# RWKV time mix: where a chunk's group norm is finished, which engine scales the state, and how the output projection is cut

## The chip, the core and the metric

One core of one Trainium2 chip runs the whole program in one launch. Its engines work side by side, each through a queue of its own in order: TensorE (PE, with its weight loads shown apart as PEld), VectorE (DVE), ScalarE (ACT), GpSimd (POOL) and SyncE (SP), which issues the DMAs. The metric is the device time of one execution in microseconds; the median of three runs is 2095.94 us.

## The reference, cut to what matters

The program is a stack of four layers over 256 tokens of width 1024. The change lies in the second layer's mixer, an RWKV-7 time mix with 16 heads of 64:

```python
def step(state, inp):
    r_t, w_t, k_t, v_t, kk_t, a_t = inp
    sa = jnp.einsum('bhvk,bhk->bhv', state, -kk_t)
    state = (state * w_t[:, :, None, :]
             + sa[..., None] * (kk_t * a_t)[:, :, None, :]
             + v_t[..., None] * k_t[:, :, None, :])
    y = jnp.einsum('bhvk,bhk->bhv', state, r_t)
    return state, y
...
mean = jnp.mean(y, axis=-1, keepdims=True)
var = jnp.mean(jnp.square(y - mean), axis=-1, keepdims=True)
yn = ((y - mean) * lax.rsqrt(var + LNX_EPS)).reshape(B, S, D)
yn = yn * lnx_w.astype(f32) + lnx_b.astype(f32)
bonus = (jnp.sum(r * k * r_k.astype(f32), axis=-1, keepdims=True) * v).reshape(B, S, D)
return ((yn + bonus).astype(x.dtype) * g) @ w_o
```

A group norm over each head's 64 values of `y`, gain and bias, a bonus, a gate `g`, and the output projection `w_o` (1024 by 1024). Everything is fp32.

## The kernel before

Activations lie with the feature on the partitions and the token along the free axis. Weights come as blocks of 128x1024, called units, through one queue of DMAs (`Stream`); `get()` hands out the next unit. A unit is either raw, so its matmuls are plain fp32, two rows on PE each (`add32`, L662, L665), or it is split by ScalarE (L378) and VectorE (L380) into a high and a low part of a rounded type, and a product is then three single-pass matmuls, one row each (`mm3`, L592 to L597). The split buffers are three; a unit's buffer goes back when the next unit is taken.

The recurrence is done in four chunks of 64 tokens (`rwkv_core`). `chain(c, fill)` (L1352) is the serial part. It multiplies the state `UV` by the queries of the correction (L1365) and copies the result to `Rs` (L1366, the first four head pairs on ScalarE, the rest on VectorE), solves within the chunk (L1378, copied to `UV` by L1380, half of the partitions on either engine), forms the next state (L1385, copied by L1388, which adds the old state scaled by the chunk's decay) and the outputs `y` (L1375, L1395), which ScalarE copies to `ym` (L1396). The scaled state `p0` is two multiplies of GpSimd (L1370), for chunks 1 and 2 alone, since chunk 0 starts from nothing and chunk 3 passes nothing on.

`outs(c, ym, zm)` (L1402) is the group norm of a chunk, in three steps: `center` (a matmul with the centring matrix, L1411; the square on ScalarE, L1412; the product with gate and gain on VectorE, L1413), `variance` (small matmuls, L461; an addition on VectorE, L1420; a power on GpSimd, L1422; a copy that spreads it, on ScalarE, L1423) and `scale` (four transposes, L1428; product and additions on VectorE, L1429 to L1438; a split of the upper half of the features, L566, L567). `chain` calls pieces of `fill` at three places (`more`): after the state's update, after the output matmuls, and after the last of those. So the group norm of chunk c - 1 runs beside chunk c, all three steps of it; that of chunk 3 runs after it in two halves. The tiles `ym`, `zm` and the scaled keys share the name `ymem` and its two buffers.

The projection follows. Its first four units are raw and go through twice, with tokens 0 to 191 and then 192 to 255; the other four are split and go through once with all 256 tokens, in the order of the units. All eight accumulate in four PSUM banks (`Acc`, L648). Each output feature block gets, per unit, a matmul of the given tokens (fp32) or three (single-pass). The tile framework sets the order on each engine from the order of the code and its own priorities; what it made is shown with the change.

Of the kernel before, what the change touches and what calls it, by code (L numbers as in the profile page):

```python
# [10 lines left out]
F32 = mybir.dt.float32  # L11
# [4 lines left out]
OP = mybir.AluOpType  # L16
# [3 lines left out]
P = 128  # L20
T = 256
# [122 lines left out]
def stream_units(inp):  # L144
# [15 lines left out]
    def qk(h):  # L160
        add(2048, lambda: _colunit(np.concatenate([wqkv[0][:, h * P:(h + 1) * P], wqkv[0][:, D + h * P:D + (h + 1) * P]], 1), 0))

    def v(j):
        add(2048, lambda: _colunit(wqkv[0], 2048 + 256 * j))
# [4 lines left out]
    for h in range(10):  # L169
        if h < 7:  # L170
            qk(h + 1)
        if h == 0:
            v(2)
            v(3)
        if h > 1:
            add(1024, lambda: wo[0][(h - 2) * P:(h - 1) * P])
# [276 lines left out]
def psum(k, tag, name=None):  # L453
    return k.ps.tile([P, 512], F32, name=tag, bufs={"acc": 4, "mm": 2, "tp": 2}[tag])
# [37 lines left out]
class Stat:  # L492
# [34 lines left out]
    def cols(self, tag="tp"):  # L527

        k, nc = self.k, self.k.nc
        if self.rs is not None:  # L530
            return self.rs
        if self.sums:
            self.i = self.n - len(self.sums)
            for x in self.sums:
                self.product(x, tag)
        while self.i < self.n:
            self.feed(self.h[:, self.i])
        m = self.m
        ms = k.small.tile([P, 2 * m], F32, name=f"ms{m}")
        nc.vector.tensor_scalar(ms[:, 2 * m - 2:], self.ps[:, 0:2 * m:m], 1e-6, None, op0=OP.add)  # L540
        if m == 2:

            nc.vector.scalar_tensor_tensor(ms[:, 0:2], ms[:, 2:4], 1e-6, self.ps[:, 1:4:2], op0=OP.mult, op1=OP.add)
        rs = k.small.tile([P, 2 * m], F32, name=f"rs{m}")
        nc.gpsimd.tensor_tensor(rs, ms, k.mh[:, 0:2 * m], op=OP.pow)
        self.rs = rs
        return rs
# [44 lines left out]
def mm3(k, out, w, x, start, stop, **kw):  # L592

    nc = k.nc
    nc.tensor.matmul(out, w[0], x[0], start=start, stop=False, **kw)  # L595
    nc.tensor.matmul(out, w[0], x[1], start=False, stop=False, **kw)  # L596
    nc.tensor.matmul(out, w[1], x[0], start=False, stop=stop, **kw)  # L597
# [50 lines left out]
class Acc:  # L648
# [3 lines left out]
        self.k, self.n, self.i = k, n, 0  # L652
        self.ps = [psum(k, "acc") for _ in range(4)]

    def add(self, unit, x):
        for m in range(8):
            w = [u[:, m * P:(m + 1) * P] for u in unit]
            mm3(self.k, self.ps[m // 2][:, (m % 2) * T:(m % 2 + 1) * T], w, x,
                self.i == 0 and m % 2 == 0, self.i == self.n - 1, skip_group_check=True)
        self.i += 1  # L660

# [318 lines left out]
def own(e):  # L980

    return slice(64 * e, 64 * e + 64)


def oth(e):

    return slice(64 - 64 * e, 128 - 64 * e)
# [250 lines left out]
def rwkv_core(k, h, es, R):  # L1238
    nc = k.nc
    pool = k.pool("rw_core", es=es)  # L1240
    flat = lambda t: t.rearrange("p a b -> p (a b)")
    t8 = lambda t: t.rearrange("p (h t) -> p h t", t=64)
    UV = pool.tile([P, 4, 8, 2, 64], F32, name="UV")
# [44 lines left out]
        GR.append(g)  # L1288

    def keys(c):  # L1290
        bk = pool.tile([P, 8, P], F32, name="ymem", bufs=2)
        for hp in range(8):
            nc.scalar.activation(bk[:, hp], R.BK[:, hp, c], AF.Copy, scale=R.PC[:, hp, c:c + 1])
        bt = pool.tile([P, 8, P], F32, name="BT", bufs=3)
        for half in range(2):
            ps = psum(k, "mm")
            for i in range(4):
                nc.tensor.transpose(ps[:, i * P:(i + 1) * P], bk[:, half * 4 + i], k.ident)
            nc.scalar.copy(bt[:, half * 4:half * 4 + 4], ps.rearrange("p (a t) -> p a t", a=4))
        BT.append(bt)  # L1300
# [23 lines left out]
    for c in range(4):  # L1324
        steps[c][0]()
        if c < 3:
            keys(c)
        if c < 2:
            spread_values(c + 2)
# [11 lines left out]
    def gate(j):  # L1341
        pg = psum(k, "mm")
        for m in range(2):
            hp = 2 * j + m
            nc.tensor.matmul(pg[:, m * T:(m + 1) * T], g2[:, hp * P:(hp + 1) * P], R.G1, start=True, stop=True)
            nc.scalar.activation(GL[:, hp], pg[:, m * T:(m + 1) * T], AF.Copy, scale=k.V("lnw", hp))
        nc.vector.tensor_tensor(flat(BG[:, 2 * j:2 * j + 2]), flat(BG[:, 2 * j:2 * j + 2]), pg, op=OP.mult)

    heads = [(hp, e) for hp in range(8) for e in range(2)]
    o = [None]  # L1350

    def chain(c, fill):  # L1352
        fill = iter(fill)
        more = lambda: [f() for f in next(fill, ())]
        cols = lambda hp: slice(hp * 64, hp * 64 + 64)
        Rs = pool.tile([P, 8, 64], F32, name="Rs")
        sides = [(half, slice(4 * half, 4 * half + 4), heads[8 * half:8 * half + 8]) for half in range(2)]
        at = lambda hp: cols(hp % 4)
        t4 = lambda x: t8(x)[:, 0:4]
        py = []  # L1360
        for half, hs, hd in sides:
            pr = psum(k, "acc")
            for hp, e in hd:
                r = oth(e) if c == 0 else slice(0, P)
                nc.tensor.matmul(pr[own(e), at(hp)], R.GTA[r, hp, c, e], UV[r, c, hp, e], start=True, stop=True)  # L1365
            both(half)(Rs[:, hs], t4(pr))  # L1366
        if 0 < c < 3:
            p0 = pool.tile([P, 8, 64], F32, name="PS0")
            for e in range(2):
                nc.gpsimd.tensor_tensor(p0[own(e)], UV[own(e), c, :, e], R.PC[own(e), :, c:c + 1].to_broadcast([64, 8, 64]), op=OP.mult)  # L1370
        for half, hs, hd in sides:
            py.append(psum(k, "acc"))
            if c > 0:
                for hp, e in hd:
                    nc.tensor.matmul(py[-1][own(e), at(hp)], UV[own(e), c, hp, e], R.RT[own(e), hp, c], start=hp % 4 == 0, stop=False, skip_group_check=True)  # L1375
            pu = psum(k, "acc")
            for hp, e in hd:
                nc.tensor.matmul(pu[own(e), at(hp)], XF[own(e), c * 8 + hp], Rs[own(e), hp], start=True, stop=True)  # L1378
            for e in range(2):
                both(e)(UV[own(e), c, hs, e], t4(pu)[own(e)])  # L1380
        if c < 3:
            for half, hs, hd in sides:
                ps = psum(k, "acc")
                for hp, e in hd:
                    nc.tensor.matmul(ps[own(e), at(hp)], BT[c][:, hp, own(e)], UV[:, c, hp, e], start=True, stop=True)  # L1385
                for e in range(2):
                    if c > 0:
                        nc.vector.tensor_tensor(UV[own(e), c + 1, hs, e], t4(ps)[own(e)], p0[own(e), hs], op=OP.add)  # L1388
                    else:
                        both(e)(UV[own(e), c + 1, hs, e], t4(ps)[own(e)])  # L1390
        more()
        ym = pool.tile([P, 2, 512], F32, name="ymem", bufs=2)
        for half, hs, hd in sides:
            for hp, e in hd:
                last = nc.tensor.matmul(py[half][own(e), at(hp)], UV[:, c, hp, e], GR[c][:, hp, e], start=c == 0, stop=True, skip_group_check=True)  # L1395
            nc.scalar.copy(ym[:, 0, half * 256:half * 256 + 256], py[half][:, 0:256])  # L1396
        more()
        with k.tc.issue_after(last.ins):
            more()
        return ym  # L1400

    def outs(c, ym, zm, h0=0, h1=8):  # L1402
# [37 lines left out]

        return center, variance, scale

    zmem = lambda: pool.tile([P, 2, 512], F32, name="ymem", bufs=2)
    ym = chain(0, [[lambda: gate(0), lambda: gate(1)], [lambda: gate(2), lambda: gate(3)]])
    k.st.free()
    for c in range(1, 4):
        f = outs(c - 1, ym, zmem())
        ym = chain(c, [[x] for x in f])
    zm = zmem()
    for f in zip(outs(3, ym, zm, 0, 4), outs(3, ym, zm, 4, 8)):  # L1450
        for x in f:
            x()

    acc = Acc(k, 12)
    us = [k.st.get() for _ in range(4)]
    for hp in range(4):
        acc.add32(us[hp], o[0][0][:, hp], slice(0, 192))
    for hp in range(4):
        acc.add32(us[hp], o[0][0][:, hp], slice(192, T))
        k.st.free(us[hp])  # L1460
    for hp in range(4, 8):
        acc.add(k.st.get(), [x[:, hp - 4] for x in o[0][1:]])
    return partial(acc.residual, h)


# [758 lines left out]
```

## Time and profile before

| | |
|---|---|
| runs | 2095.38, 2095.94, 2096.98 us |
| profiled execution | 2096.53 us, span 2094.7 us |
| PE busy | 2047.3 us (98%), 13856 matmuls |
| PEld busy | 1804.7 us (86%) |
| DVE busy | 1695.8 us (81%) |
| ACT busy | 1284.0 us (61%) |
| POOL busy | 134.3 us (6%) |
| mean granted clock of PE | 0.991 |

Times within the span count from its start. A busy time is the union of an engine's instructions; PE's rows overlap, since matmuls are pipelined, so what a matmul costs in a stream is the distance between starts, not its length. The granted clock is 1.00 at 2.4 GHz and 0.50 at 1.2 GHz. Idle time of an engine is put down to what ended it. The stretch of the change runs from about 485 to 562 us of the span.

### The profile page before, as it was taken

The page shows a single profiled execution, that of the slowest core. Times are in us where ns is not written, and L with a number is a line of the kernel's source. Part 1 is how long each engine was busy: PE and PEld are TensorE (multiplying, and loading weights), DVE is VectorE, ACT ScalarE, POOL GpSimd, SP SyncE. Part 2 cuts the span into 40 slices and gives each one's busy share as a digit, 9 for nine tenths or more (in the row PEclk, how much of TensorE's full clock was granted, in tenths as well). Part 3 has the DMA queues.
Part 4 walks back from the last instruction along what each step waited for, and adds up shares of the span by engine and source line. Part 5 has one row for each costly group of instructions (what it writes and reads, how often), then busy time and mean ns, then how long its engine had stood idle before and what let it go on. Part 6 is the DMA issues. An engine that isn't in the chain of part 4 may idle for free.

```text
span 2094.7 us, 36233 instructions
## 1 busy us (share of the span) xinstructions
PE 2047.3 (98%) x13856; PEld 1804.7 (86%) x13856; DVE 1695.8 (81%) x2417; ACT 1284.0 (61%) x1833; POOL 134.3 (6%) x133
## 2 busy tenths in 40 slices
PE   8999999998999999999999999999999999999997
PEld 7889998887899988999998878888888888887875
DVE  6879876665499767598877489999998989888987
ACT  6665453534364556454456477777777777777775
POOL 1011111101011100100000110000000000000002
PEclk9999999999999999999999999999999999999998
DMA  7348752230588634588854489998999999999991
GB/s 297 131 170 292 263 171 71 92 121 33 196 293 315 205 102 167 192 304 327 308 221 144 141 306 355 346 359 311 371 346 370 316 364 355 359 337 353 365 353 64
DMA packets 147910, 533.48 MB, mean 255 GB/s; under 512 B 16784, under 2 KB 17040, under 8 KB 147600
## 3 DMA queue, kind: packets, MB, share of 16 engines
q1 hardware_dynamic: 147728, 531.08, 69.6%
q8 instruction: 111, 1.82, 0.3%
q14 instruction: 71, 0.58, 0.1%
HBM read 529.97 MB, written 1.05 MB: 254 GB/s over the span
## 4 chain that ended last, share of the span: by engine, by line
PE 53%; DVE 3%; ACT 1%; issue 1%; DMA 0%; POOL 0%; ACTq 0%; POOLq 0%
PE acc L1958 8%; PE acc L1959 8%; PE acc L1957 8%; PE mm L1992 4%; PE mm L1991 4%; PE mm L1994 4%; PE mm L641 2%; PE acc L596 2%; PE acc L597 2%; PE acc L595 2%; DVE wlo L380 1%; PE mm L595 1%; PE mm L596 1%; PE mm L597 1%; PE tp L596 1%; PE tp L597 1%
## 5 line engine op out<-in xcount | busy, mean ns | idle before, releaser
L380 DVE TENSOR_TENSOR wlo<-raw,whi 128x1024 fp32r<-128x1024 f32 (+1 forms) x602 | 726.8, 1225 | 113.7 <-ACT whi L378 103.3
L378 ACT CAST whi<-raw 128x1024 fp32r<-128x1024 f32 (+1 forms) x608 | 622.6, 1041 | 249.3 <-PE acc L596 73.1
L1958 PE MATMUL acc<-wlo,XE 128*128 128x512 f32 x768 | 303.4, 395 | 1.0
L1957 PE MATMUL acc<-whi,XE 128*128 128x512 f32 x768 | 302.4, 395 | 0.0
L1959 PE MATMUL acc<-whi,XE 128*128 128x512 f32 x768 | 302.0, 393 | 0.0
L595 PE MATMUL mm<-Ahi,whi 128*128 128x256 f32 (+1 forms) x1016 | 290.8, 286 | 1.4 <-ACT whi L378 1.3
L597 PE MATMUL mm<-Ahi,wlo 128*128 128x256 f32 (+1 forms) x1016 | 289.0, 284 | 1.7 <-DVE wlo L380 1.7
L596 PE MATMUL mm<-Alo,whi 128*128 128x256 f32 (+1 forms) x1016 | 288.4, 284 | 0.7 <-DVE Alo L589 0.6
L595 PEld LDWEIGHTS mm<-Ahi,whi 128*128 128x128 f32 x1016 | 193.3, 190 | 4.9 <-issue 2.3
L597 PEld LDWEIGHTS mm<-Ahi,wlo 128*128 128x128 f32 x1016 | 193.2, 190 | 4.1 <-DVE wlo L380 2.2
L596 PEld LDWEIGHTS mm<-Alo,whi 128*128 128x128 f32 x1016 | 193.2, 190 | 1.7 <-DVE Alo L589 1.1
L380 DVE TENSOR_TENSOR wlo<-more,whi 128x1024 fp32r<-128x1024 f32 x150 | 177.8, 1219 | 9.6 <-ACT whi L378 6.8
L1958 PEld LDWEIGHTS acc<-wlo,XE 128*128 128x128 f32 x768 | 144.3, 188 | 37.4 <-DVE wlo L380 7.0
L378 ACT CAST whi<-more 128x1024 fp32r<-128x1024 f32 x150 | 154.3, 1049 | 33.5 <-PE acc L1959 22.2
L1957 PEld LDWEIGHTS acc<-whi,XE 128*128 128x128 f32 x768 | 144.4, 188 | 31.0
L1959 PEld LDWEIGHTS acc<-whi,XE 128*128 128x128 f32 x768 | 144.3, 188 | 30.5
L596 PE MATMUL acc<-fs,whi 128*128 128x256 f32 x544 | 152.6, 281 | 0.9 <-DVE fs L567 0.8
L597 PE MATMUL acc<-fs,wlo 128*128 128x256 f32 x544 | 152.9, 282 | 0.0
L595 PE MATMUL acc<-fs,whi 128*128 128x256 f32 x544 | 152.1, 282 | 0.4 <-ACT fs L566 0.4
L1992 PE MATMUL mm<-whi,h 128*128 128x512 f32 x384 | 152.1, 396 | 0.0
L1991 PE MATMUL mm<-whi,h 128*128 128x512 f32 x384 | 151.4, 394 | 0.0
L908 DVE SCALAR_TENSOR_TENSOR adaw<-adaw,adac 128x1024 f32<-128x1024 f32 x96 | 122.2, 1275 | 18.2 <-DMA adaw<-ada 17.8
(502 smaller groups left out, 3838.3 us busy)
## 6 DMA issues: line engine op xcount, KB each, us to landing
raw<-ws SPq DMA_DIRECT2D x658, 512.0 KB, 4.9
more<-ws SPq DMA_DIRECT2D x150, 512.0 KB, 5.7
adaw<-ada SPq DMA_DIRECT2D x96, 512.0 KB, 5.9
con<-ws SPq DMA_DIRECT2D x27, 512.0 KB, 5.5
tables<-ws SPq DMA_DIRECT2D x26, 512.0 KB, 5.6
rows<-ws SPq DMA_DIRECT2D x25, 512.0 KB, 5.6
XE<-ws SPq DMA_DIRECT2D x10, 512.0 KB, 5.1
raw<-ws SPq DMA_DIRECT2D x12, 256.0 KB, 5.2
```

The costliest lines, as they stand in the source:

```text
L378: self.ins[n] = nc.scalar.copy(hi[:, s], raw[:, s]).ins
L380: self.last = eng.tensor_tensor(lo[:, s], raw[:, s], hi[:, s].bitcast(F32), op=OP.subtract).ins
L595: nc.tensor.matmul(out, w[0], x[0], start=start, stop=False, **kw)
L596: nc.tensor.matmul(out, w[0], x[1], start=False, stop=False, **kw)
L597: nc.tensor.matmul(out, w[1], x[0], start=False, stop=stop, **kw)
L908: nc.vector.scalar_tensor_tensor(x, x, 1.0, c, op0=OP.mult, op1=OP.mult, accum_out=raw[:, j:j + 1])
L1957: nc.tensor.matmul(ps, xe[0][:, kt], w[0], start=(kt == 0), stop=False)
L1958: nc.tensor.matmul(ps, xe[0][:, kt], w[1], start=False, stop=False)
L1959: nc.tensor.matmul(ps, xe[1][:, kt], w[0], start=False, stop=(kt == KT - 1))
L1991: nc.tensor.matmul(py[e][q], x[0][i], w[0][i], start=(c == 0 and f + i == 0), stop=False)
L1992: nc.tensor.matmul(py[e][q], x[1][i], w[0][i], start=False, stop=False)
L1994: end = nc.tensor.matmul(py[e][q], x[0][i], w[1][i], start=False, stop=(c == 5 and f + i == 3))
```

## The change

`scale` of chunk c - 1 moves from the end of chain c to the first `more` of chain c + 1, ahead of `center` of chunk c; `scale` of chunk 2 follows chain 3, ahead of the group norm of chunk 3. The third place of `more` in `chain` goes. The two multiplies of L1370 go from GpSimd to VectorE. The tiles named `ymem` get a third buffer. In the projection the first seven units, four raw and three split, go through twice, with tokens 0 to 127 and then 128 to 255; the eighth goes once with all 256. For this `add` gets a slice of tokens, and the buffers of the three split units are taken out of the stream's hands (`kept`) and given back after their second pass. The four accumulators and the units' order are the same.

```diff
-    def add(self, unit, x):
+    def add(self, unit, x, s=slice(0, T)):
         for m in range(8):
             w = [u[:, m * P:(m + 1) * P] for u in unit]
-            mm3(self.k, self.ps[m // 2][:, (m % 2) * T:(m % 2 + 1) * T], w, x,
+            mm3(self.k, self.ps[m // 2][:, (m % 2) * T + s.start:(m % 2) * T + s.stop], w, [v[:, s] for v in x],
...
-        bk = pool.tile([P, 8, P], F32, name="ymem", bufs=2)
+        bk = pool.tile([P, 8, P], F32, name="ymem", bufs=3)
...
-                nc.gpsimd.tensor_tensor(p0[own(e)], UV[own(e), c, :, e], R.PC[own(e), :, c:c + 1].to_broadcast([64, 8, 64]), op=OP.mult)
+                nc.vector.tensor_tensor(p0[own(e)], UV[own(e), c, :, e], R.PC[own(e), :, c:c + 1].to_broadcast([64, 8, 64]), op=OP.mult)
...
         more()
-        with k.tc.issue_after(last.ins):
-            more()
         return ym
...
+    scale = []
     for c in range(1, 4):
         f = outs(c - 1, ym, zmem())
-        ym = chain(c, [[x] for x in f])
+        ym = chain(c, [scale + [f[0]], [f[1]]])
+        scale = [f[2]]
+    scale[0]()
     zm = zmem()
...
-    acc = Acc(k, 12)
-    us = [k.st.get() for _ in range(4)]
-    for hp in range(4):
-        acc.add32(us[hp], o[0][0][:, hp], slice(0, 192))
-    for hp in range(4):
-        acc.add32(us[hp], o[0][0][:, hp], slice(192, T))
-        k.st.free(us[hp])
-    for hp in range(4, 8):
-        acc.add(k.st.get(), [x[:, hp - 4] for x in o[0][1:]])
+    acc = Acc(k, 15)
+    us, kept = [k.st.get() for _ in range(4)], []
+    for _ in range(3):
+        us.append(k.st.get())
+        kept.append(k.st.spl.pop(k.st.cur - 1))
+    for s in (slice(0, P), slice(P, T)):
+        for hp in range(7):
+            if hp < 4:
+                acc.add32(us[hp], o[0][0][:, hp], s)
+            else:
+                acc.add(us[hp], [x[:, hp - 4] for x in o[0][1:]], s)
+            if s.start and hp < 4:
+                k.st.free(us[hp])
+            elif s.start:
+                t = kept.pop(0)
+                k.st.free_spl[t[0]].append(t)
+    acc.add(k.st.get(), [x[:, 3] for x in o[0][1:]])
```

The order on PE in chunk 2, before (-) and with the change (+). L1428, now L1426, are the transposes of a chunk's `scale`, L1411, now L1409, the centring, L1378 the products with `Rs`, L1385 the next state, L1395 the outputs:

```order
 L1375 MATMUL acc<-Ahi,UV 64x64 x8
-L1378 MATMUL acc<-Rs,xa 64x64 x5
-L1428 MATMUL tp<-ident,ymem 128x128 x4
-L1378 MATMUL acc<-Rs,xa 64x64 x3
+L1378 MATMUL acc<-Rs,xa 64x64 x8
 L1375 MATMUL acc<-Ahi,UV 64x64 x8
 L1378 MATMUL acc<-Rs,xa 64x64 x8
 L1385 MATMUL acc<-UV,BT 64x64 x8
-L1411 MATMUL mm<-ymem,con 128x512
-L1395 MATMUL acc<-GR,UV 64x64 x9
+L1426 MATMUL tp<-ident,ymem 128x128 x4
+L1409 MATMUL mm<-ymem,con 128x512
```

The four transposes of chunk 0 stood between the products with `Rs`, and stand behind the first half of the next state now.

The order on PE behind the last outputs of chunk 3, before, where L461 are the variances' small matmuls and L665 the fp32 matmuls of the projection:

```order
-L1411 MATMUL mm<-ymem,con 128x256 x2
-L1428 MATMUL tp<-ident,ymem 128x128 x4
-L461 MATMUL tp<-con,ymem 64x2 x8
-L665 MATMUL acc<-xv,raw_86 128x192
-L1428 MATMUL tp<-ident,ymem 128x128 x2
-L665 MATMUL acc<-xv,raw_86 128x192 x5
-L1428 MATMUL tp<-ident,ymem 128x128 x2
```

And the same place with the change:

```order
+L1409 MATMUL mm<-ymem,con 128x256 x2
+L665 MATMUL acc<-xv,raw_86 128x128 x4
+L1426 MATMUL tp<-ident,ymem 128x128 x4
+L461 MATMUL tp<-con,ymem 64x2 x4
+L665 MATMUL acc<-xv,raw_86 128x128 x4
+L461 MATMUL tp<-con,ymem 64x2 x4
+L665 MATMUL acc<-xv,raw_87 128x128 x3
+L1426 MATMUL tp<-ident,ymem 128x128 x2
+L665 MATMUL acc<-xv,raw_87 128x128 x3
+L1426 MATMUL tp<-ident,ymem 128x128 x2
```

The projection's first matmuls stood behind the transposes of chunk 2, and stand ahead of them now, with three more groups between the steps of chunk 3.

The order on VectorE in chunk 2. L1418 is the variance's addition, L1366 the copy to `Rs`, L1380 a copy of solved values, L380 a unit's low part:

```order
+L1418 TENSOR_SCALAR var<-tp 128x8
+L1370 TENSOR_TENSOR PS_5520<-UV,PC 64x512
 L1366 COPY Rs<-acc 128x256
-L1429 TENSOR_TENSOR ymem<-ymem,tp 128x512
+L1370 TENSOR_TENSOR PS_5520<-UV,PC 64x512
 L1380 COPY UV<-acc 64x4x64
-L1435 TENSOR_TENSOR xv<-ymem,BK 128x4x64
-L1438 TENSOR_TENSOR ymem<-ymem,BK 128x256
 L380 TENSOR_TENSOR wlo_91<-raw_89,whi_90 128x1024
+L1380 COPY UV<-acc 64x4x64
+L1388 TENSOR_TENSOR UV<-acc,PS_5520 64x4x64 x2
```

The state's two multiplies stand on either side of the copy to `Rs`, and chunk 0's product and additions have left the place ahead of the solved values. On SyncE's queue the order of the DMAs is the same.

## Rows read from the trace of the kernel before

**Rows 1.** Windows: us, busy PE, PEld, DVE, ACT, POOL, then clock, DMA share, GB/s
```profile
494.60:502.80 8.20, 7.82 (x181) 6.24 (x182) 4.40 (x8) 3.84 (x9) 0.19 (x1) 1.00 0.19 68
502.80:515.65 12.85, 9.30 (x187) 7.67 (x186) 7.02 (x16) 4.49 (x10) 3.74 (x3) 0.87 0.23 79
515.65:524.00 8.35, 6.79 (x158) 5.41 (x154) 5.48 (x12) 3.94 (x8) 1.64 (x1) 1.00 0.03 9
524.00:529.60 5.60, 2.63 (x25) 1.95 (x24) 2.39 (x7) 1.82 (x5) 2.08 (x2) 0.92 0.54 187
529.60:550.73 21.13, 21.00 (x135) 20.39 (x133) 3.45 (x10) 1.52 (x4) 1.68 (x2) 0.86 0.15 52
```

**Rows 2.** PE timeline, chunk 2: start us, length us, instruction, idle before
```profile
505.22 0.51 PE L1378 MATMUL acc<-Rs,xa 64*64 64x64 f32 x10
508.67 1.11 PE L1428 MATMUL tp<-ident,ymem 128*128 128x128 f32 x4 [2.94 <-ACT ymem L1423]
...
511.89 0.69 PE L1385 MATMUL acc<-UV,BT 128*64 128x64 f32 x16
```

**Rows 3.** Timeline of GpSimd (POOL) in chunk 2
```profile
504.08 2.16 POOL L1370 TENSOR_TENSOR PS<-UV,PC 64x512 f32<-64x512 f32 x2 [9.29 <-DVE UV L1388]
506.33 1.64 POOL L1422 TENSOR_TENSOR yrs<-var,mh 128x8 f32<-128x8 f32 x1
```

**Rows 4.** Timelines of VectorE (DVE) and ScalarE (ACT) in chunk 2
```profile
504.58 0.16 DVE L1420 TENSOR_SCALAR var<-tp 128x8 f32<-128x8 f32 x1
...
508.00 0.62 ACT L1423 COPY ymem<-yrs 128x512 f32<-128x512 f32 x1 [4.01 <-POOL yrs L1422]
```

**Rows 5.** Windows around the two falls of the clock, as rows 1
```profile
508.67:510.70 2.03, 2.03 (x22) 1.70 (x24) 0.69 (x1) 0.27 (x1) 0.00 (x0) 0.50 0.00 0
524.00:527.57 3.57, 1.14 (x6) 0.68 (x5) 1.05 (x3) 1.32 (x4) 1.64 (x1) 1.00 0.60 197
527.57:534.60 7.03, 6.35 (x35) 5.52 (x36) 3.52 (x10) 1.61 (x5) 2.12 (x2) 0.58 0.13 51
```

**Rows 6.** Timeline of PE, chunk 3 and the start of the projection
```profile
519.60 0.66 PE L1428 MATMUL tp<-ident,ymem 128*128 128x128 f32 x4 [1.42 <-ACT ymem L1423]
...
524.80 1.13 PE L1411 MATMUL mm<-ymem,con 128*128 128x256 f32 x4 [0.79 <-ACT ymem L1396]
527.57 0.66 PE L1428 MATMUL tp<-ident,ymem 128*128 128x128 f32 x4 [1.63 <-ACT ymem L1423]
528.15 0.40 PE L461 MATMUL tp<-con,ymem 128*64 128x2 f32 x8
...
529.62 1.01 PE L665 MATMUL acc<-xv,raw 128*128 128x192 f32 x2
...
531.24 3.41 PE L665 MATMUL acc<-xv,raw 128*128 128x192 f32 x10
```

**Rows 7.** Line L665 in two windows: rows, ns min/median/max, first and last start
```profile
L665 PE MATMUL acc<-xv,raw x48: 326/326/326, 535.7 to 543.3; 128*128 128x192 f32 x48
L665 PE MATMUL acc<-xv,raw x59: 275/275/275, 543.8 to 550.3; 128*128 128x64 f32 x59
```

**Rows 8.** Lines L596 and L1958, every third single-pass matmul, as rows 7
```profile
L596 PE MATMUL acc<-xb,whi x25: 283/283/283, 552.0 to 560.6; 128*128 128x256 f32 x25
L1958 PE MATMUL acc<-wlo,XE x11: 388/394/397, 1500.9 to 1507.8; 128*128 128x512 f32 x11
```

**Rows 9.** Weight loads (PEld) of the same two kinds, as rows 7
```profile
L665 PEld LDWEIGHTS acc<-xv,raw x59: 192/192/192, 543.9 to 550.4; 128*128 128x128 f32 x59
L596 PEld LDWEIGHTS acc<-xb,whi x26: 192/192/192, 551.9 to 560.9; 128*128 128x128 f32 x26
```

**Rows 10.** Timeline of VectorE in chunk 1
```profile
495.45 0.69 DVE L1347 TENSOR_TENSOR BK<-BK,mm 128x512 f32<-128x512 f32 x1 [1.92 <-ACT BK L1346]
```

**Rows 11.** Timelines of GpSimd and VectorE at the same moment, in the tail
```profile
531.69 1.01 POOL L1422 TENSOR_TENSOR yrs<-var,mh 128x4 f32<-128x4 f32 x1 [1.42 <-DVE var L1420]
...
531.94 0.42 DVE L1435 TENSOR_TENSOR xv<-ymem,BK 128x256 f32<-128x256 f32 x1
```

More of the change, by code (lines that the diff above doesn't have):

```diff
@@ L1391, in chain @@
         more()
-        ym = pool.tile([P, 2, 512], F32, name="ymem", bufs=2)
+        ym = pool.tile([P, 2, 512], F32, name="ymem", bufs=3)
         for half, hs, hd in sides:
@@ L1441, in outs @@
         return center, variance, scale
-    zmem = lambda: pool.tile([P, 2, 512], F32, name="ymem", bufs=2)
+    zmem = lambda: pool.tile([P, 2, 512], F32, name="ymem", bufs=3)
     ym = chain(0, [[lambda: gate(0), lambda: gate(1)], [lambda: gate(2), lambda: gate(3)]])
     k.st.free()
+    scale = []
     for c in range(1, 4):
         f = outs(c - 1, ym, zmem())
-        ym = chain(c, [[x] for x in f])
+        ym = chain(c, [scale + [f[0]], [f[1]]])
+        scale = [f[2]]
+    scale[0]()
     zm = zmem()
```

## The prediction, made before the changed kernel ran

> **What bounds the kernel now.** I read the page first: PE is busy for 98% of the span, so time comes only from places where PE stands still, runs at its lower clock, or has work that can be made shorter. Then the windows view, cut at the edges of the chunks of the recurrence and of the projection behind it [rows 1]. Chunk 1 takes 8.20 us, chunk 2 takes 12.85 and chunk 3 8.35, for the same number of matmuls, so 4 to 5 us of chunk 2 are a stall. Behind chunk 3 come 5.60 us with PE busy for 2.63, then the projection: 21.13 us of fp32 matmuls and 96 single-pass ones of 256 columns, 11.4 us at the pitch below.
>
> The timeline of PE names the stall of chunk 2: four transposes wait 2.94 us for ScalarE's copy, in the middle of the matmuls with `Rs` [rows 2]. GpSimd's timeline says why the copy is late: the power of chunk 0 runs from 506.33, behind two multiplies of 1.08 us each [rows 3], though its input left VectorE at 504.74 [rows 4]. The stall costs twice: after it the granted clock is 0.50 for 2.03 us [rows 5], so 1.2 GHz in place of 2.4. The same happens at the end: the transposes of chunk 2 wait 1.63 us, the first fp32 matmul of the projection starts at 529.62 [rows 6], and the clock averages 0.58 over the 7.03 us from those transposes on [rows 5]. Inside chunk 3 a wait of 1.42 us has the same cause [rows 6].
>
> Last, the pitch of the projection's matmuls (first start to last start). An fp32 matmul is two rows of PE. At 192 columns a row takes (543.3 - 535.7)/47 = 0.162 us, at 64 columns (550.3 - 543.8)/58 = 0.112 us [rows 7]. A third of the columns takes 70% of the time: something other than the columns bounds the narrow row. Single-pass matmuls: 256 columns take (560.6 - 552.0)/72 = 0.119 us (24 gaps of every third row), 512 columns (1507.8 - 1500.9)/30 = 0.230 us [rows 8].
>
> **The change, part by part.** I walk PE's new order with durations from these rows; each start is the later of the engine being free and the last input being ready.
>
> *Chunk 2.* GpSimd's two multiplies go, so the power starts at about 504.8 and ends 1.64 us later [rows 3], ScalarE's copy of 0.62 us [rows 4] ends near 507.2, and its copies of the solved values, queued behind it, let the state update start at about 508.0 in place of 511.89 [rows 2]. The transposes come after the first half of that update, where their input is ready, so nothing waits for them. A wait of some 1.4 us before the state update is what is left. From there to the end of the chunk the same matmuls took 3.76 us (511.89 to 515.65) [rows 1, 2], and the transposes add 0.6 [rows 6]. Chunk 2 comes to 9.5 us: **-3.35**.
>
> *VectorE's four new multiplies.* No row shows them there. The nearest is a multiply of as many elements a partition, 0.69 us [rows 10]; GpSimd's 1.08 [rows 3] is the other end. I take 0.69. In chunk 1 the pair lies in 1.92 us in which VectorE waits for ScalarE [rows 10]. In chunk 2 one stands ahead of VectorE's `Rs` copy and one behind; the copy comes 0.7 us later, when PE is still at the first half's matmuls, and the second ends near 506.7, before ScalarE's copy at 507.2. So they cost nothing; at 1.08 us each the second would end near 507.3 and still cost nothing. VectorE's second copy now stands behind a weight subtraction that waits for ScalarE's cast; it ends near 510.2, when PE is at the centring of chunk 1.
>
> The page "SBUF — State Buffer" of the Trainium skill (section "Who interferes with whom") says that a VectorE instruction with two SBUF inputs and a GpSimd instruction that reads SBUF shut each other out, which would put the second multiply behind the power and make chunk 2 about 0.7 us longer, the sum -4.15. Here a VectorE addition with two SBUF inputs ran its usual 0.42 us inside GpSimd's power of 1.01 us [rows 11], so the row speaks against it, and I leave it out.
>
> *Chunk 3.* The transposes of chunk 1 stand after the centring of chunk 2, so PE works where it waited 1.42 us [rows 6]. New: VectorE's `Rs` copy and the two halves of the solved values come behind more of its own work, about 0.25 us of waits, while the 6.79 us of busy PE [rows 1] hold some 0.2 that is chunk 2's. I take 6.8 in place of 8.35: **-1.55**.
>
> *Tail and fp32 part.* Before: 524.00 to 550.73, or 26.73 us [rows 1]. Now the first pass needs only chunks 0 and 1, and its fp32 matmuls stand between the last chunk's small steps. An fp32 matmul of 128 columns is bounded below by 256 stream steps of 0.162/384 = 0.108 us a row and by the narrow row's 0.112; I take 0.112, the larger, so 32 matmuls are 32 x 0.224 = 7.2 us a pass. Pass one: centring 1.1 [rows 6], matmuls 7.2, transposes and variances 1.9 (0.6, twice 0.3 and twice 0.35, by the rows of four and of eight at full clock [rows 6]), and waits of about 1.9 (the transposes of chunk 2 still wait 1.5 us, since four matmuls cover only 0.9 of a chain that takes 2.6 from variance to copy, and the first half of chunk 3 waits 0.4): 12.1. Pass two: 7.2. Together 19.3: **-7.45**. Of this 3.2 us are a better split (192 + 64 columns cost 0.324 + 0.224 a matmul, 128 + 128 cost 0.448); the rest are covered waits and the lower clock, during which twelve rows ran at 0.33 us [rows 6].
>
> *Single-pass part.* Three units are done twice with 128 columns: 144 matmuls for 72, and the last unit stays whole. This price decides, and no row before shows a single-pass matmul under 256 columns. Columns alone, from 0.119 and 0.230, give 0.064 us; the price of an fp32 matmul of that width, two rows, gives 0.224. I take 0.112, that of the 64-column fp32 row: it streams as long (64 columns at two steps), it loads as wide a weight, and the weight load takes 192 ns in both forms [rows 9]. So 144 x 0.112 = 16.1 against 72 x 0.119 = 8.6: **+7.5**. The halving buys nothing in these units.
>
> *At nothing:* the third `ymem` buffer (the keys of chunks 0 to 2 are scaled earlier, while PE has other work) and the later free of the three kept units: the last unit's split waits for the first of them, which comes two units of 24 x 0.112 and one of 24 x 0.119 before the end, 8.3 us, where it is 8.6 now. What is late next is the same first unit of the feed-forward.
>
> Sum: -3.35 - 1.55 - 7.45 + 7.5 = **-4.85 us**. The same walk with the order of before gives 528.4 for the first fp32 matmul, where the trace has 529.62: it leaves out the lower clock. So it holds to about 1.2 us at each end of the path. The profiled execution took 2096.53 us (span 2094.7); less 4.85 is 2091.7. It lies 0.6 above the median of the three runs, 2095.94, so the median to expect is **2091.1 us**. A measurement of this kernel can tell about 0.2%, 4.2 us, from no change; the forecast lies just beyond.
>
> **The rivals.**
> 1. *Narrow single-pass matmuls cost as much as fp32 ones.* Were a 128-column one to take 0.224 us, 144 of them cost 16.1 us more than I allow: +11.3, so 2107.2. It decides from 0.112 + 4.85/144 = 0.146 us upward. For it: the code keeps every narrow piece in fp32, and the trace is silent. Against: it is one row of PE at 256 and 512 columns, and follows the columns there [rows 8]. Chance 0.17.
> 2. *The floor of 0.112 belongs to fp32 alone*, and single-pass rows follow the columns: 0.064, a further -6.9, so 2084.2. Against it: equal weight-load rows [rows 9]. Chance 0.09.
> 3. *The cover fails.* The waits left in the tail (1.5 and 0.4 us) or the 1.4 of chunk 2 let the clock fall as now: as long as in the present tail, 6.8 us at half, costs 3.4; so 2094.5, no change. For it: two of three such stretches before had it. Against: PE did 1.14 us of work in the 3.57 before that fall [rows 5], and would do over half now; the wait of 1.42 in chunk 3 had no fall behind it. Chance 0.15.
> 4. *Weight loads do not lie beside a running matmul.* A load of 0.112 and a stream of 0.054 would add up to 0.166 us, +7.8, so 2098.9. The 64-column row has both parts and takes 0.112 [rows 7], so hardly. The page "TensorE: Matmul & The Clock Gate" of the Trainium skill (section "The mechanism") says that a weight load overlaps matmuls in flight only when the row group differs, which is this; the trace disagrees. Chance 0.03.
>
> That the change does not do what it says is out: the order shows every move.
>
> **How the numbers follow.** The forecast has 0.56 and its own range is 2088 to 2094 (1.2 us at either end of the walk, narrow rows between 0.105 and 0.120). Somewhat over half of it lies beyond 4.2 us: 0.31 faster, 0.25 same. Rival 2 adds 0.09 to faster, rival 3 gives 0.13 to same and 0.02 to slower, rivals 1 and 4 give 0.20 to slower. Faster 0.40, same 0.38, slower 0.22. For 8 in 10 the range must reach rival 1; rival 2 is left out: 2087 to 2108.
>
> **What would show it.** Chunk 2 from its first matmul to that of chunk 3 near 9.5 us, with no wait of PE for chunk 0's transposes; GpSimd with powers alone; the first fp32 matmul of 128 columns within 1.5 us of chunk 2's variance; a granted clock of 1.00 through the tail; rows of 0.112 us in both kinds of pass. Single-pass rows over 0.146 make the forecast wrong in sign, rows near 0.064 make it too small, a clock of 0.50 behind the tail's first wait is rival 3.

## The result and the profile after

| | before | after |
|---|---|---|
| median of 5 runs each, us | 2095.42 (2090.98 to 2096.98) | 2104.87 (2104.69 to 2109.65) |
| ratio, 95% interval | | 1.0057 [1.0046, 1.0069] |
| span of the profiled execution, us | 2094.7 | 2103.1 |
| mean granted clock | 0.991 | 0.987 |

The changed kernel is slower by 9.45 us, where 4.85 less were forecast. First the place that the forecast was about: the windows view of the changed kernel, cut at the same edges as [rows 1] (chunks 1, 2 and 3; the rest of the tail with the first fp32 pass; the first single-pass pass; the second fp32 pass; the second single-pass pass; the last unit). The columns are those of [rows 1].

```profile
508.45:517.60 9.15, 7.86 (x181) 6.25 (x182) 4.81 (x9) 4.40 (x11) 0.00 (x0) 1.00 0.19 61
517.60:526.95 9.35, 7.28 (x187) 6.15 (x185) 7.22 (x15) 3.07 (x6) 1.94 (x1) 1.00 0.31 101
526.95:533.95 7.00, 6.92 (x157) 5.54 (x155) 6.01 (x14) 3.88 (x9) 1.75 (x1) 1.00 0.26 95
533.95:545.80 11.85, 10.57 (x94) 9.64 (x93) 6.08 (x18) 3.75 (x10) 3.75 (x3) 1.00 0.14 46
545.80:553.80 8.00, 8.00 (x74) 8.00 (x74) 0.00 (x0) 0.00 (x0) 0.00 (x0) 1.00 0.01 2
553.80:561.00 7.20, 7.20 (x67) 7.20 (x66) 0.00 (x0) 0.00 (x0) 0.00 (x0) 1.00 0.49 151
561.00:568.95 7.95, 7.95 (x74) 7.95 (x73) 2.46 (x2) 2.10 (x2) 0.00 (x0) 1.00 0.86 308
568.95:571.95 3.00, 3.00 (x27) 2.96 (x25) 1.95 (x4) 1.87 (x3) 0.00 (x0) 1.00 0.65 212
```

These add up to 63.50 us. Before, the same work took 67.73: 56.13 from chunk 1 to the first single-pass matmul [rows 1], and 11.60 for the four single-pass units behind it. So 4.23 us are gained here, close to the forecast, at a granted clock of 1.00 throughout. The loss lies ahead of it. Chunk 1 starts at 508.45 in place of 494.60, behind the solves and queries (64x64 matmuls, L1265 and L461) and the keys. `keys(c)` makes a chunk's keys ready: ScalarE scales them into a `ymem` tile (eight instructions, L1293), PE transposes that (L1298), and ScalarE copies the result to `BT` (L1299). The windows of that stretch, first of the changed kernel, then of the one before:

```profile
457.35:460.00 2.65, 2.65 (x40) 2.56 (x40) 0.00 (x0) 2.65 (x10) 0.00 (x0) 1.00 0.53 196
460.00:465.15 5.15, 2.12 (x35) 1.81 (x33) 2.51 (x3) 5.04 (x15) 0.00 (x0) 1.00 0.00 1
466.10:500.20 34.10, 34.10 (x482) 32.11 (x480) 11.09 (x15) 5.38 (x11) 0.00 (x0) 0.50 0.01 2
500.20:508.45 8.25, 8.25 (x135) 6.68 (x134) 5.62 (x11) 6.72 (x18) 0.00 (x0) 1.00 0.01 2
```

```profile
459.70:465.15 5.45, 4.77 (x73) 4.37 (x72) 2.29 (x3) 5.36 (x16) 0.00 (x0) 1.00 0.27 96
465.15:494.60 29.45, 29.43 (x622) 26.16 (x622) 16.15 (x25) 14.97 (x40) 1.92 (x2) 1.00 0.01 3
```

From the first solve to chunk 1 the changed kernel takes 508.45 - 457.35 = 51.10 us, before 494.60 - 459.70 = 34.90: **16.2 us lost**. In 34.10 of the 51.10 us TensorE is busy all the time at a granted clock of 0.50, its level of 1.2 GHz. What came first is in the timeline of PE (changed kernel, then before; of this and the later timelines only the rows spoken of are shown):

```profile
460.23 1.90 PE L1265 MATMUL tp<-xa,Alo 64*64 64x64 f32 x32
465.16 1.25 PE L1298 MATMUL mm<-ident,ymem 128*128 128x128 f32 x8 [3.04 <-ACT BT L1299]
466.34 3.31 PE L1265 MATMUL tp<-xa,Alo 64*64 64x64 f32 x32
...
498.30 2.06 PE L1345 MATMUL mm<-G,raw 128*128 128x256 f32 x4
```

```profile
462.58 1.90 PE L1265 MATMUL tp<-xa,Alo 64*64 64x64 f32 x32
465.17 1.15 PE L1298 MATMUL mm<-ident,ymem 128*128 128x128 f32 x8 [0.70 <-ACT BT L1299]
466.25 1.90 PE L1265 MATMUL tp<-xa,Alo 64*64 64x64 f32 x32
```

The second chunk's key transposes wait 3.04 us for ScalarE in place of 0.70; behind the wait the same 32 matmuls take 3.31 us in place of 1.90, and the clock rises only near 500 us, at the end of the first matmuls with a 128x128 weight and 256 columns (L1345, in `gate`). ScalarE's timeline (changed kernel, then before) says why:

```profile
457.10 4.78 ACT L1293 ACTIVATE ymem<-BK,PC 128x128 f32<-128x128 f32 x16
461.90 0.59 ACT L1336 COPY vt<-acc 128x512 f32<-128x512 f32 x1
464.52 1.08 ACT L1299 COPY BT<-mm 128x512 f32<-128x512 f32 x2
```

```profile
459.45 2.45 ACT L1293 ACTIVATE ymem<-BK,PC 128x128 f32<-128x128 f32 x8
461.91 0.59 ACT L1336 COPY vt<-acc 128x512 f32<-128x512 f32 x1
464.53 1.08 ACT L1299 COPY BT<-mm 128x512 f32<-128x512 f32 x2
465.48 1.00 ACT L1293 ACTIVATE ymem<-BK,PC 128x128 f32<-128x128 f32 x3
```

With two `ymem` buffers the third chunk's keys had to wait for a buffer, so their eight scalings stood behind the first copies to `BT`. With three they are ready at once and stand ahead: 16 in one block, 2.3 us more before the copy that PE waits for.

The account: PE was 2.35 us earlier at the first solve in the changed kernel. Of this it had 0.73 at 331 us already (the same 64 matmuls of L461 start at 330.98 and, before, at 331.71); the rest comes from a stretch at half clock near 335 us, which the profiled execution of before has and this one has not (windows 320 to 340: 0.91 and 1.00). -2.35 + 16.2 - 4.23 is +9.6 us at the projection's end; the spans differ by 8.4, so 1.2 us come back behind it.

### The profile page after: what moved, and what is told of

It is laid out like the page before. It is cut to its first block, busy times and chain, and to the rows that moved or that the text cites. A ratio compares the mean times of both kernels' runs of the same rounds, so it can differ in the third digit from the quotient of the medians.

```text
span 2103.1 us, 36364 instructions
## 1 busy us (share of the span) xinstructions
PE 2057.2 (98%) x13928; PEld 1815.9 (86%) x13928; DVE 1700.3 (81%) x2421; ACT 1282.9 (61%) x1833; POOL 129.1 (6%) x129
## 5 line engine op out<-in xcount | busy, mean ns | idle before, releaser
L380 DVE TENSOR_TENSOR wlo<-raw,whi 128x1024 fp32r<-128x1024 f32 (+1 forms) x602 | 727.2, 1226 | 115.9 <-ACT whi L378 106.3
L596 PE MATMUL mm<-Alo,whi 128*128 128x256 f32 (+1 forms) x1016 | 288.0, 284 | 0.7 <-DVE Alo L589 0.6
L596 PEld LDWEIGHTS mm<-Alo,whi 128*128 128x128 f32 x1016 | 192.7, 190 | 1.7 <-DVE Alo L589 1.1
L380 DVE TENSOR_TENSOR wlo<-more,whi 128x1024 fp32r<-128x1024 f32 x150 | 177.9, 1220 | 9.6 <-ACT whi L378 6.8
L596 PE MATMUL acc<-fs,whi 128*128 128x256 f32 x544 | 152.7, 281 | 0.9 <-DVE fs L567 0.8
```

The costliest lines, as they stand in the source:

```text
L380: self.last = eng.tensor_tensor(lo[:, s], raw[:, s], hi[:, s].bitcast(F32), op=OP.subtract).ins
```

## The experiments

The theory: **the third buffer puts the third chunk's scalings ahead of the copy to `BT`; PE waits 3 us; the clock falls, and the 64x64 matmuls that follow do not bring it back.** The rivals: the narrow passes of the projection or VectorE's multiplies cost the time; the buffer itself does it in some other way; the long half clock came by chance. Times are medians; the kernel before ran beside each group: 2095.01 us (e1 to e4), 2094.82 (e5 to e8), 2094.16 (e9 to e11).

**e1_keys_two.** The keys rotate through two buffers; `ym` and `zm` take those in turn with a third of their own.

```diff
-        bk = pool.tile([P, 8, P], F32, name="ymem", bufs=3)
+        bk = pool.tile([P, 8, P], F32, name="ymem", bufs=2)
-        ym = pool.tile([P, 2, 512], F32, name="ymem", bufs=3)
+        ym = zmem()
-    zmem = lambda: pool.tile([P, 2, 512], F32, name="ymem", bufs=3)
+    third = [0]
+
+    def zmem():
+        third[0] += 1
+        if third[0] % 3 == 0:
+            return pool.tile([P, 2, 512], F32, name="ymx")
+        return pool.tile([P, 2, 512], F32, name="ymem", bufs=2)
```

> The changed kernel with the keys kept to two buffers as before: the third buffer goes only to the chain's outputs. Theory (the third buffer lets ScalarE scale two chunks of keys in one block, PE waits 3.04 us for BT, the clock falls to 0.50 and stays there for 34 us): no half clock between 465 and 500 us of the span, chunk 1 starts again near 494.6 us, and what is left of the change gains 4 to 5 us: about 2091 us. Rival (the narrow passes of the projection or VectorE's multiplies cost the time): as the changed kernel, about 2105 us. Rival (the long half clock came by chance and hangs on nothing in the kernel): either, with 2105 as likely as 2091.

Measured: 2090.69 us (2089.15 to 2093.28), ratio 0.9985 [0.9976, 0.9994]. The wait for `BT` is 0.71 us, and the windows show no half clock:

```profile
464.47 1.15 PE L1298 MATMUL mm<-ident,ymem 128*128 128x128 f32 x8 [0.71 <-ACT BT L1299]
```

```profile
457.70:466.00 8.30, 7.59 (x94) 6.54 (x93) 2.70 (x3) 8.17 (x24) 0.00 (x0) 1.00 0.24 89
466.00:500.00 34.00, 33.96 (x736) 29.49 (x736) 20.51 (x33) 15.88 (x42) 0.00 (x0) 1.00 0.06 18
```

Without the third buffer for the keys the change gives 4.3 us; 14.2 of the changed kernel's time hang on that one number.

**e2_third_buffer_alone.** The kernel before with `bufs=3` for `ymem` in its three places.

> The kernel before with the third ymem buffer and nothing else: 16 scalings of keys in one block on ScalarE. Theory: PE waits about 3 us for BT near 465 us, the granted clock is 0.50 from there for about 34 us, and the time is 12 to 16 us over before: 2107 to 2112 us. Rival (it is the projection or the multiplies): no change, 2095 us. Rival (chance): either.

Measured: 2111.55 us (2107.76 to 2112.86), ratio 1.0077 [1.0063, 1.0091]: 16.5 us lost. PE's timeline row of the wait, and the window behind it:

```profile
467.64 1.97 PE L1298 MATMUL mm<-ident,ymem 128*128 128x128 f32 x8 [3.06 <-ACT BT L1299]
```

```profile
467.20:504.70 37.50, 37.06 (x507) 34.77 (x508) 11.43 (x17) 7.42 (x15) 0.00 (x0) 0.50 0.01 2
```

All five executions take over 2107 us, where none of the kernel before takes over 2098, so it is not chance.

**e3_projection_alone.** The kernel before with the changed projection (and `add` with its slice), nothing else.

> The kernel before with the changed projection alone (seven units in two passes of 128 tokens), two buffers, group norm as before. Theory: the tail and the fp32 units gain about 7, the single-pass units cost 7.5: within 1 us of before, 2095 to 2097 us, clock 1.00 between 465 and 500. Rival (the projection is what cost the time): 2103 to 2106 us.

Measured: 2096.11 us (2093.60 to 2099.51), ratio 1.0010 [1.0001, 1.0019]. The narrow passes are not what cost 9 us; what they win in the fp32 units goes in the single-pass ones, about as the forecast's two terms had it (-7.45 and +7.5). In its trace the stretch from chunk 1 to the last single-pass matmul takes 69.1 us in place of 67.6, and the tail still has half clock (0.87 over 13.05 us from 522.50).

**e4_group_norm_alone.** e1 with the projection of before (`Acc(k, 12)`, 192 and 64 tokens, single-pass units whole).

> The moved group norm and VectorE's multiplies alone, keys in two buffers, projection as before (192 and 64 tokens, single-pass units whole). Theory: chunk 2 and chunk 3 gain 3.35 and 1.55 us, the tail is about as before: 2090 to 2092 us. Rival (the multiplies on VectorE or the later group norm cost more than they give): 2096 us or over.

Measured: 2088.07 us (2086.72 to 2089.73), ratio 0.9971 [0.9960, 0.9982]: 6.9 us, 2 more than expected. From chunk 1 to the last single-pass matmul its trace takes 61.8 us, before 67.6, so 5.8 are gained there, though the tail still has half clock (0.61 over 8.00 us from 518.00). Its profiled execution also lacks the half clock near 335 us, whose 3.4 us cost at most 1.7. The median of e1, which has the changed projection besides, is 2.6 us higher, and its trace takes 62.9 us for the stretch: on top of the moved group norm the projection as changed costs time (the two intervals overlap a little).

**e5_single_pass_whole.** e1 with the two passes for the fp32 units alone.

```diff
+    acc = Acc(k, 12)
+    us = [k.st.get() for _ in range(4)]
+    for s in (slice(0, P), slice(P, T)):
+        for hp in range(4):
+            acc.add32(us[hp], o[0][0][:, hp], s)
+            if s.start:
+                k.st.free(us[hp])
+    for hp in range(4, 8):
+        acc.add(k.st.get(), [x[:, hp - 4] for x in o[0][1:]])
```

> As e1_keys_two, but the four single-pass units are done whole, 256 columns a matmul; only the four fp32 units keep the two passes of 128. Theory (a single-pass matmul of 128 columns costs nearly as much as one of 256, so halving it buys nothing): 144 x 0.110 us become 72 x 0.119, 7.3 us less than e1: 2083 to 2084 us, 11 to 12 us under before. Rival (the three units in the first pass are needed as cover for the tail): the tail waits again, half of the gain is lost: 2087 us or over.

Measured: 2081.67 us (2081.18 to 2082.34), ratio 0.9935 [0.9923, 0.9948]: 13.2 us under before. Its windows of the tail with both fp32 passes, and of all four single-pass units:

```profile
519.85:538.60 18.75, 17.67 (x159) 16.73 (x157) 5.29 (x16) 3.39 (x10) 3.75 (x3) 1.00 0.27 87
538.60:550.20 11.60, 11.60 (x99) 11.59 (x97) 4.37 (x6) 3.96 (x5) 0.00 (x0) 1.00 0.77 267
```

The changed kernel takes 11.85 + 7.20 = 19.05 us for the first and 8.00 + 7.95 + 3.00 = 18.95 for the second. The single-pass units were not needed as cover: the fp32 pass of 128 tokens is enough.

**e6_keys_on_two_engines.** The changed kernel with three buffers, every second scaling of the keys on VectorE (`tensor_scalar`, L1294).

> The changed kernel with its third buffer kept, and every second scaling of the keys on VectorE, so that ScalarE has 4 where it had 8 ahead of BT. Theory (what lowers the clock is PE's wait for ScalarE, not the buffer as such): no wait over 1 us between 455 and 475 us, clock 1.00 through the solves, 2088 to 2092 us. Rival (the third buffer, or chance, or the projection): half clock from about 465 us, 2103 to 2107 us.

Measured: 2089.05 us (2087.98 to 2092.33), ratio 0.9972 [0.9961, 0.9983]. The timelines of VectorE and PE, and a window:

```profile
452.41 2.44 DVE L1294 TENSOR_SCALAR ymem<-BK,PC 128x128 f32<-128x128 f32 x12
464.13 1.09 PE L1301 MATMUL mm<-ident,ymem 128*128 128x128 f32 x8
```

```profile
460.00:500.00 40.00, 39.75 (x853) 35.26 (x850) 23.46 (x37) 20.17 (x48) 0.00 (x0) 1.00 0.10 29
```

Three buffers, no wait, no half clock: it is the wait and not the buffer as such.

**e7_full_matmuls_inside.** The changed kernel, with this behind `queries(0)`:

```diff
+        if c == 0:
+            px = psum(k, "mm")
+            for i in range(4):
+                nc.tensor.matmul(px[:, (i % 2) * T:(i % 2 + 1) * T], k.ident, R.BK[:, 2 * i:2 * i + 2, 0], start=True, stop=True)
```

> The changed kernel with four more fp32 matmuls of 128 rows, 128 weight columns and 256 columns (their result is not used) behind the first chunk's queries, inside the stretch at half clock, near 477 us. Theory (the clock stays low because 64x64 matmuls fill a quarter of the array, and full matmuls bring it back, as the first ones at 498 us do in the changed kernel): they take about 4.1 us, and the clock is 1.00 behind them; the 19 us that are left of the stretch take 9.5: about 5.4 us less than the changed kernel, 2099 to 2100 us, and the half clock lasts 15 to 18 us in place of 34. Rival (its length is set by time or by the wait alone): half clock to about 502 us, 4 us over the changed kernel, 2109 us.

Measured: 2107.07 us, but in two groups: 2099.24, 2102.45, 2103.15 and 2110.98, 2111.79, 2112.77; ratio 1.0058 [1.0038, 1.0079]. The profile is of the run of 2103.15: the added matmuls, and the windows up to and behind the rise of the clock.

```profile
483.13 3.78 PE L1336 MATMUL mm<-BK,ident 128*128 128x256 f32 x8
```

```profile
467.00:487.45 20.45, 19.95 (x190) 17.87 (x191) 4.54 (x6) 4.94 (x9) 0.00 (x0) 0.50 0.01 2
487.45:500.00 12.55, 12.55 (x331) 11.64 (x329) 7.35 (x11) 2.33 (x6) 0.00 (x0) 1.00 0.01 3
```

In this execution the clock rose 0.5 us behind the last of the full matmuls, and the 64x64 matmuls after them ran at 1.00. The upper group lies 2 to 4 us above the 2109 of the rival, but none of it was profiled, so this run alone settles nothing.

**e8_wait_with_two_buffers.** The kernel before, in which the loop over `c == 1` scales its keys twice.

> The kernel before, two buffers, with the second chunk's keys scaled twice (same result), so that ScalarE does 16 scalings in one block ahead of BT, as in the changed kernel, without a third buffer. Theory (the wait alone does it): PE waits about 3 us for BT, half clock for some 34 us from about 467 us, 2107 to 2112 us, as e2. Rival (the third buffer itself, not the wait): the extra 2.44 us of ScalarE cost at most 2.4 us: 2095 to 2098 us.

Measured: 2113.65 us (2111.57 to 2117.86), ratio 1.0094 [1.0081, 1.0107]. ScalarE's row, PE's row and the window:

```profile
459.74 4.78 ACT L1294 ACTIVATE ymem<-BK,PC 128x128 f32<-128x128 f32 x16
467.80 1.97 PE L1299 MATMUL mm<-ident,ymem 128*128 128x128 f32 x8 [3.04 <-ACT BT L1300]
```

```profile
467.30:504.80 37.50, 37.00 (x488) 34.16 (x488) 11.45 (x16) 8.94 (x22) 0.00 (x0) 0.50 0.01 2
```

2.44 us more on ScalarE cost 18.8 us. The same wait makes the same stretch without a third buffer.

**e9_twice_the_full_matmuls.** e7 with `range(8)`.

> As e7_full_matmuls_inside with eight such matmuls in place of four. e7 gave two groups of times, 2099 to 2103 and 2111 to 2113 us, and its profile, of a run of 2103, showed the clock rise at the end of the four. Theory (full matmuls bring the clock back, and four are only just enough, so that some executions stay low): with eight every execution rises; the added four take 2 to 4 us: 2101 to 2106 us, none near 2112, half clock 18 to 24 us. Rival (the rise in e7's profile was chance): two groups again, or all near 2113 to 2117 us.

Measured: 2102.08 us (2098.96 to 2103.60), ratio 1.0041 [1.0027, 1.0055]; all five runs lie at the lower group, none near the upper.

```profile
480.99 4.86 PE L1336 MATMUL mm<-BK,ident 128*128 128x256 f32 x16
```

```profile
466.00:483.00 17.00, 17.00 (x181) 15.67 (x180) 4.16 (x5) 4.06 (x8) 0.00 (x0) 0.51 0.01 2
483.00:500.00 17.00, 17.00 (x378) 15.36 (x377) 7.34 (x11) 3.58 (x10) 0.00 (x0) 0.99 0.01 3
```

The clock rose in the middle of the eight, near 483 us, where the changed kernel's rose near 500, at the end of its own first 128x256 matmuls (L1345). With work that is thrown away the median lies 2.8 us under that of the changed kernel, though the two intervals overlap. That the upper group of e7 is executions in which four came short is only argued, from its times.

**e10_multiplies_on_gpsimd.** e1 with `nc.gpsimd` in line 1370.

> As e1_keys_two, with the four multiplies of the state's scaling back on GpSimd. Theory (in chunk 2 they stand ahead of the power, 1.6 us): the power and ScalarE's copy come 1.6 us later, PE's wait before the state update grows from 1.57 us to about 3.1: 2092 to 2093 us, and up to 2096 if that wait brings half clock with it. Rival (the moved group norm alone hides it): no difference, 2090 to 2091 us.

Measured: 2092.10 us (2090.00 to 2095.94), ratio 0.9993 [0.9984, 1.0002]. GpSimd's timeline in chunk 2, PE's wait before the state update, and the window behind it:

```profile
503.74 2.17 POOL L1370 TENSOR_TENSOR PS<-UV,PC 64x512 f32<-64x512 f32 x2 [9.17 <-DVE UV L1388]
505.98 1.64 POOL L1420 TENSOR_TENSOR yrs<-var,mh 128x8 f32<-128x8 f32 x1
509.11 1.12 PE L1385 MATMUL acc<-UV,BT 128*64 128x64 f32 x16 [2.77 <-DVE UV L1380]
```

```profile
508.00:514.70 6.70, 5.59 (x55) 3.97 (x57) 3.62 (x6) 2.35 (x5) 0.00 (x0) 0.54 0.26 82
```

The power stands behind the multiplies again, the wait is 2.77 us where e1 has 1.57, and in the profiled execution (2095.07) the clock falls at its end. The intervals of e10 and e1 overlap, so the times do not show the 1.4 us between the medians; the profile alone speaks for them.

**e11_both_remedies.** e6 with the projection of e5.

> The changed kernel with its third buffer kept, keys' scalings on two engines as in e6_keys_on_two_engines, and the single-pass units whole as in e5_single_pass_whole. Theory (the two are independent): e6 less 7.3 us: 2081 to 2083 us, as e5 or a little below, since PE's wait of 0.70 us for BT goes too. Rival (VectorE's twelve scalings are in the way of something): over 2084 us.

Measured: 2079.88 us (2076.66 to 2080.99), ratio 0.9927 [0.9914, 0.9941]: 14.3 us under before and 25 under the changed kernel. It is the best version here.

## Why the prediction was wrong

The step that failed is a clause: "*At nothing:* the third `ymem` buffer (the keys of chunks 0 to 2 are scaled earlier, while PE has other work)". PE had other work for 4.8 us (2.65 and 2.12 in the windows); ScalarE had no time to spare, being busy for 5.04 of the 5.15 us up to the end of PE's wait. Earlier scalings could only push back what stood behind them, and that was the copy to `BT`, for which PE already waited 0.70 us. Measured by itself (e2), the clause is worth +16.5 us. Of the 16.2 us in the trace 3.04 - 0.70 = 2.3 are the wait; the other 13.9 are the half clock. The third rival had this mechanism, but looked for it in the tail and chunk 2, behind waits that were already in view, and priced it at 3.4 us.

Every priced term but chunk 1 held in the trace of the changed kernel, by its own steps:

- Chunk 2: 9.5 forecast, 9.35 measured, with a wait of 1.48 us before the state update (1.4), and GpSimd with powers alone.
- VectorE's multiplies: 0.67 and 0.69 us each (0.69), nothing late behind them. On GpSimd they make PE's wait 1.2 us longer (e10); that the time differs is not shown beyond the noise.
- Chunk 3: 6.8 forecast, 7.00.
- Tail and first pass 12.1, second pass 7.2; measured 11.85 and 7.20, clock 1.00. The transposes of chunk 2 wait 0.74 us, where 1.5 was forecast:

```profile
535.45 1.05 PE L665 MATMUL acc<-xv,raw 128*128 128x128 f32 x8
537.24 0.66 PE L1426 MATMUL tp<-ident,ymem 128*128 128x128 f32 x4 [0.74 <-ACT ymem L1421]
545.92 0.28 PE L596 MATMUL acc<-xb,whi 128*128 128x128 f32 x1
551.95 0.28 PE L596 MATMUL acc<-xb,whi 128*128 128x128 f32 x1
```

- Single-pass rows of 128 columns: (551.95 - 545.92)/54 = 0.112 us, as taken from [rows 7]; 15.95 us against the 16.1 of the forecast. Rivals 1, 2 and 4 fall with that. The narrow row is not set by its columns, whose share is 0.054 by the stream step of [rows 7]. The page "TensorE: Matmul & The Clock Gate" of the Trainium skill (section "LDWEIGHTS (loading the stationary operand)") has a weight load take its columns over 1.2 in ns, by my estimate 0.107 us for 128; the rows agree with a pitch bound by the load, beside which the running matmul lies. That the load is what binds stays argued: no run here changes the width of the weight alone, and the records of a load show 0.192 us [rows 9], more than the pitch.
- Chunk 1 was taken as unchanged and took 9.15 us in place of 8.20: a cast of ScalarE ahead of the centring's square waited 2.52 us for its DMA (1.60 before), and PE 1.25 for the square (0.26). e1 has 8.00, and e9, with three buffers, 7.65 (505.64 to 513.29), so this is the meeting of queues, not the edit.

The sum of the terms is -4.23 in the trace and -4.7 in that of e1, against -4.85. The forecast is e1's time: 2091.1 against 2090.69. So close a match is in part luck: in e1 chunk 3 takes 7.85 us, with waits of 0.86 for VectorE's `Rs` copy and 0.42 for the transposes, where 6.8 was forecast, and chunk 1 and the tail make up for it.

By edit the sum splits otherwise than by place. The terms of the moved group norm (-3.35 and -1.55) add up to -4.9, and alone it gave 6.9 us (e4); the terms of the tail and the projection (-7.45 and +7.5) add up to nothing, and by the medians the changed projection cost 1.1 us alone (e3) and 2.6 on top of the moved group norm (e1 over e4). The clock of 1.00 in the tail, which the term of -7.45 counts, came only with both: the tail of either alone still has half clock.

Two readings of the prediction need a word. The 2.03 us at 0.50 [rows 5] are a part of the half clock in chunk 2: 12.85 us at a mean of 0.87 [rows 1] make 3.3 us of it. And the measured 2104.87 us lie within the range of 2087 to 2108, but its upper end was put there for rival 1, which did not come.

## What to carry to other kernels

A buffer added in a pool that several loops share is an edit to each of them: list every instruction that it frees to run earlier, the engine it runs on, and what then stands behind it there; "earlier" is free only on an engine that has idle time. A wait is priced by the work that follows it: behind waits of 2.94 and 2.77 us in the chain the half clock lasted 3.3 us (before, from [rows 1]) and at least 6.2 (e10, 6.70 us at a mean of 0.54), ahead of the stretch of 64x64 matmuls 34 to 37. And cutting a matmul's columns pays only as far as the row is bound by columns: here 192 + 64 to 128 + 128 paid (e5 lies 6.4 us under e4, the better clock of the tail included), 256 to 128 + 128 did not (e1 lies 9.0 us over e5).

## What was not expected of the hardware

- TensorE busy for 34.10 of 34.10 us with 64x64 matmuls and a few transposes stayed at 1.2 GHz, while the same matmuls ran at 2.4 GHz throughout where the wait before them was 0.71 us (e1: 1.00 from 466 to 500). Matmuls with a full 128x128 weight and 256 columns were under way or just done when it rose (L1345 in the changed kernel, the added ones in e7 and e9); in e10 the centring's matmul with a full weight and 512 columns (L1409, 511.07 to 512.98) did not raise it at once: it stayed at 0.50 up to 515.20. The Trainium skill, page "TensorE: Matmul & The Clock Gate", section "What's actually happening", says that activity releases the throttle; these rows show that an engine which the profile calls busy can stay throttled. What exactly the full matmuls bring was not separated.
- VectorE's multiplies and GpSimd's power ran beside each other in chunk 2. VectorE's kept their length, the power took 1.94 us where it takes 1.64 without a multiply beside it ([rows 3], and e10 above):

```profile
519.42 0.67 DVE L1370 TENSOR_TENSOR PS<-UV,PC 64x512 f32<-64x512 f32 x1
520.46 0.69 DVE L1370 TENSOR_TENSOR PS<-UV,PC 64x512 f32<-64x512 f32 x1
519.66 1.94 POOL L1420 TENSOR_TENSOR yrs<-var,mh 128x8 f32<-128x8 f32 x1 [101.52 <-DVE var L1418]
```

  The rule on two SBUF inputs that the prediction weighed and left out (the Trainium skill, page "SBUF — State Buffer", section "Who interferes with whom") has at most this much in it here: 0.30 us on GpSimd's side, not the 0.7 of a full exclusion. In e1 a VectorE subtraction with two SBUF inputs (L380, 514.08, 1.23 us) lies within a power that takes 1.64 us (513.87), so two such inputs alone do not lengthen it; what sets the multiplies apart was not tested.
